# Gate and up projections in three plain passes, stage by stage, and a mixer input read row tile by row tile

## The chip, the cores and the metric

The kernel runs on one core of one Trainium2 chip. The metric is the device time of one execution in microseconds (us). Before the change it is 1038.3 us, the median of three runs (1037.62 to 1040.86 us). About 0.3% of that, some 3 us, is what a measurement can tell from no change.

## What is computed

A two-layer decoder trunk in float32 on 256 tokens of width 1024. Layer 0 is a half-step feed-forward, a Mamba-2 mixer, and a half-step feed-forward; layer 1 is a half-step feed-forward, a windowed attention over keys and values that were projected once, and a half-step feed-forward; a last norm follows. Cut to what matters:

```python
def swiglu(h, w_gate, w_up, w_down):
    return (jax.nn.silu(h @ w_gate) * (h @ w_up)) @ w_down
# D_MODEL = 1024, D_FF = 2816, SEQ = 256
x = x + 0.5 * swiglu(rmsnorm(x, norm_w[layer, 0]), gate0, up0, down0)
h = rmsnorm(x, norm_w[layer, 1])
x = x + mamba2_mixer(h, ...)            # layer 0: h @ w_in is 8 x 128 rows by 41 tiles of columns
x = x + swa_sink_attention(h, ...)      # layer 1
x = x + 0.5 * swiglu(rmsnorm(x, norm_w[layer, 2]), gate1, up1, down1)
```

The four feed-forward stages are called f0, f1, f2 and f3 in the program, in the order of time: f0 before the mixer, f1 and f2 between mixer and attention, f3 at the end.

## The kernel before

Every weight matrix is cut into units of 128 x 1024 (341 of them, in one fixed order, `ORDER`). `Weights` loads them two at a time over SyncE's queue; ScalarE rounds each to the type `fp32r` (`hi`, line 144), and VectorE makes the rest of it (`lo`, line 155). `tick()` (line 370), called after each unit's matmuls, runs what is due in a list of slots and then keeps the splitting four units ahead of TensorE. The activations are split in the same way: `xs[k]` is one tile of 128 x 512 whose left half is `xh[k]`, the high part of row tile k, and whose right half is `xl[k]`, the low part. A product keeps three of the four partial products: hi x xh, hi x xl, lo x xh.

There are two ways to work through a unit of the projections:

- `wide` (line 356): for each of eight row tiles k, one matmul of 512 columns (hi against xh and xl together) and one of 256 (lo against xh), so 16 matmuls. Its halves land side by side in one PSUM bank and have to be added: ScalarE copies the right half out, VectorE adds the left half (lines 513 to 515). With `by_part` (f > 0) the eight wide matmuls come first and the eight of 256 after them.
- `unit` (line 339): 24 matmuls of 256 columns into one half bank. Without `fresh` it runs hi x xh for all k, then hi x xl for all k, then lo x xh for all k. With `fresh` it goes row tile by row tile: for each k the three products together.

`ffn` (line 479) runs f = 0 to 21. Each f does the gate unit g, the up unit u, and from f = 4 on the down unit d of f - 4, in which `rows` (line 374) does 24 matmuls of 256 columns with the operands `hh` and `hl` that ScalarE and VectorE made of gate and up. The four down units that are left come at the end; the last two of them, in `tail` (line 542), are interleaved so that `next_stage` can take each finished row tile. In `product` (line 505) all units but the program's first go through `wide`. At the start of a stage the norm's sums go through TensorE after f = 0 (line 309) and its spread to all partitions after the gate of f = 1 (line 334). In f2, the two units of the shared keys (`kA`, `kB`) stand between u and d of f = 5.

`ssm` (line 550) reads its input with 41 units: `dt`, and then four B, four C, sixteen x and sixteen z. They go through `unit` into half banks named `sb`, with `fresh` for `dt` alone. Small matmuls and transposes of the mixer are slipped in between them. `att` (line 907) reads with `unit` too, with `fresh` for its first.

Of the kernel before, what the change touches and what calls it, by code (L numbers as in the profile page):

```python
# [17 lines left out]
T = 256  # L18
# [2 lines left out]
NF = 2816 // P  # L21
LAG = 4
SLACK = 2

NORM_AT = (1, 0, 0, 0)
SCALE_AT = (0, 0, 1, 0)
# [189 lines left out]
class Trunk:  # L216
# [262 lines left out]
    def ffn(self, l, i, key, nxt):  # L479
        nc, wk = self.nc, self.fw  # L480
        self.stage_norm(key)
        accs = self.accs(f"da_{key}")
        hs = {}

        def evac(f, g, u):
            hh = self.op.tile([P, T], F32R, tag="high", name=f"hh_{key}_{f}")
            hl = self.op.tile([P, T], F32R, tag="low", name=f"hl_{key}_{f}")
            hs[f] = (hh, hl)

            def e0():  # L490
                nc.vector.tensor_tensor(g, g, self.rs, ALU.mult)
                nc.scalar.activation(g, g, AF.Silu)
                nc.vector.tensor_tensor(u, u, self.rs, ALU.mult)

            def e1():
                nc.vector.tensor_tensor(u, u, g, ALU.mult)
                nc.scalar.activation(hh, u, AF.Copy)

            def e2():
                nc.vector.tensor_tensor(hl, u, hh.bitcast(F32), ALU.subtract)  # L500

            wait = max(0, 4 - f) if key == "f0" else 2 if f == 0 else 0
            self.slots.chain(wait, [e0, e1, e2])

        def product(name, f, t):

            b = self.bank(f"{name}_{key}_{f}")
            if self.W.pos == 0:
                self.slots.at(0, lambda: nc.scalar.copy(t, b[:, 0:T]))
                self.unit((name, l, i, f), b[:, 0:T])  # L510
                return

            def add():
                nc.scalar.copy(t, b[:, T:])  # L514
                nc.vector.tensor_tensor(t, b[:, 0:T], t, ALU.add)  # L515

            self.slots.at(0, add)
            self.wide((name, l, i, f), b, by_part=f > 0)

        for f in range(NF):  # L520
            g, u = (wk.tile([P, T], F32, tag=n, bufs=4, name=f"{n}s_{key}_{f}") for n in "gu")
            product("g", f, g)
            evac_now = lambda: evac(f, g, u)
            self.slots.late(0, evac_now)
            product("u", f, u)
            if l == 1 and i == 0 and f == 0:
                self.split_k()
            if l == 1 and i == 0 and f == 5:
                self.shared_k()
            if f >= LAG:  # L530
                self.down(l, i, f - LAG, hs, accs)
        for f in range(NF - LAG, NF - 2):
            self.down(l, i, f, hs, accs)
        self.tail([(("d", l, i, f), *hs.pop(f)) for f in (NF - 2, NF - 1)], accs, nxt)
# [15 lines left out]
    def ssm(self, nxt):  # L550
# [21 lines left out]
        def half():  # L572
            if st["n"] % 2 == 0:
                st["bank"] = self.bank(f"sb{st['n']}")
            o = st["bank"][:, (st["n"] % 2) * T : (st["n"] % 2) * T + T]
            st["n"] += 1
            return o

        def conv(c, out, o, d):
            u = ubufs[st["u"] % 4]  # L580
            st["u"] += 1

            def c0():
                V.tensor_tensor(u[:, 3:], o, self.rs, ALU.mult)

            def c1():
                A.activation(out, u[:, 3:], AF.Identity, scale=self.s("convw", 3 * 24 + c), bias=self.s("convb", c))

            def c2():
                pairs = st["taps"]  # L590
                pairs.append((out, u, c))
                if len(pairs) == 1:
                    sl.late(0, taps)

            def c3():
                A.activation(out, out, AF.Silu)

            sl.chain(d, [c0, c1, c2, c3])
# [69 lines left out]
        def cb(g):  # L668
            b = side(f"cb{g}")
            nc.tensor.matmul(b[:, 0:T], B[g][:, 0:P], C[g], start=True, stop=True)  # L670
            nc.tensor.matmul(b[:, T : T + P], B[g][:, P:T], C[g][:, P:T], start=True, stop=True)

            def e():
                m = wk.tile([P, 3, P], F32, tag="cbm", name=f"cbm{g}")
                V.tensor_tensor(m[:, 0], b[:, 0:P], causal, ALU.mult)
                V.tensor_tensor(m[:, 2], b[:, T : T + P], causal, ALU.mult)
                A.copy(m[:, 1], b[:, P:T])
                CB[g] = m

            sl.at(1, e)  # L680
# [22 lines left out]
        def prep(g):  # L703

            es = [wk.tile([P, 2, 3, P], F32, tag="E", bufs=6, name=f"E{4 * g + n}") for n in range(4)]

            def p0(n):
                tok = st["tok"]
                for i in range(2):
                    h = 8 * g + 2 * n + i  # L710
                    row = CSB[h // 4][:, h % 4]
                    A.activation(es[n][:, i, 0:2], row[:, 0:T], AF.Relu, bias=tok[:, 0, h : h + 1])
                    if i == 0:
                        V.tensor_scalar(es[n][:, i, 2], row[:, T:], tok[:, 1, h : h + 1], 0.0, ALU.add, ALU.max)
                    else:
                        A.activation(es[n][:, i, 2], row[:, T:], AF.Relu, bias=tok[:, 1, h : h + 1])

            def p1():
                for e in es:
                    A.activation(e, e, AF.Exp, scale=-1.0)  # L720

            def p2(n):
                f = es[n].rearrange("p n b l -> p n (b l)")
                c = CB[g].rearrange("p b l -> p (b l)").unsqueeze(1).broadcast_to([P, 2, 3 * P])
                V.tensor_tensor(f, f, c, ALU.mult)  # L725
                M[4 * g + n] = es[n]

            sl.chain(0, [lambda: p0(0), lambda: p0(1), lambda: p0(2), lambda: p0(3), p1])
            for n in range(4):
                sl.at(5 + n + DECAY_AT[g], lambda n=n: p2(n))  # L730
# [36 lines left out]
        def evac(what, o, d):  # L767
            kind = what[0]
            if kind == "dt":
                dt_chain(o, d)  # L770
            elif kind == "z":
                zs[what[1]] = z = wk.tile([P, T], F32, tag="zs", bufs=16, name=f"zs{what[1]}")
                sl.at(d, lambda: V.tensor_tensor(z, o, self.rs, ALU.mult))
                sl.at(d + 1, lambda: A.activation(z, z, AF.Silu))
            elif kind == "x":
                xs[what[1]] = x = wk.tile([P, T], F32, tag="xs", bufs=8, name=f"xs{what[1]}")
                conv(what[1], x, o, d)
            else:
                t = wk.tile([P, T], F32, tag=kind, name=f"{kind}{what[1]}")
                (B if kind == "B" else C)[what[1]] = t  # L780
                conv((16 if kind == "B" else 20) + what[1], t, o, d)
# [3 lines left out]
        at = {w: n for n, w in enumerate(seq)}  # L785
        ins = [w for w in seq if w[0] != "so"]

        E = {w: max(3, at[ins[min(i | 1, len(ins) - 1)]] + 1) for i, w in enumerate(ins)}
# [4 lines left out]
        for hg in range(8):  # L793
            g = hg // 2
            turned[hg] = max(E["x", 2 * hg], E["x", 2 * hg + 1]) + 3 + SLACK + TURN_AT[hg]
            if hg % 2 == 0:
                start[g] = max(free, turned[hg] - 5, E["C", g] + SLACK)
                free = start[g] + 7
            ymm_at[hg] = max(turned[hg] + 2, start[g] + 7 + 2 * (hg % 2)) + MIX_AT[hg]
        for g in range(GROUPS):  # L800
            plan(E["C", g] + 3 + SLACK, lambda g=g: cb(g))
            sl.at(base + start[g] - sl.now, lambda g=g: prep(g))
# [22 lines left out]
        for what in seq[:-2]:  # L825
            if what[0] == "so":
                tt = what[1]
                if not accs:
                    accs = self.accs("sa")
                self.rows([(self.W.next(what), yh[tt], yl[tt])], accs, tt == 0, False)  # L830
                self.tick()
            else:
                o = half()
                self.unit(what, o, before=lambda: evac(what, o, E[what] - at[what]), fresh=what == ("dt",))
        self.tail([(w, yh[w[1]], yl[w[1]]) for w in seq[-2:]], accs, nxt)


# [399 lines left out]
```

## Time and profile before

| What | us |
|---|---|
| median of three runs | 1038.3 |
| the profiled execution | 1038.29 |
| its span, first to last instruction | 1036.5 |
| TensorE busy | 1013.4 |
| VectorE busy | 774.7 |
| ScalarE busy | 627.4 |
| mean granted TensorE clock | 0.995 |

Of one execution the hardware profiler gives every instruction with its engine, its line and the names that it reads and writes. PE is TensorE's matmuls, PEld its weight loads, DVE VectorE, ACT ScalarE, POOL GpSimd, SP the queue that issues the DMAs. The program ran 1.8 us longer than its span. A matmul's start is recorded, its end is modelled; so the time of a group of matmuls is read here from one group's start to the next one's, and two groups overlap by a fraction of a microsecond in the listings. The chain of waits gives a group of equal matmuls on one line, with their count.

### The profile page before, as it was taken

The page shows a single profiled execution, that of the slowest core. Times are in us where ns is not written, and L with a number is a line of the kernel's source. Part 1 is how long each engine was busy: PE and PEld are TensorE (multiplying, and loading weights), DVE is VectorE, ACT ScalarE, POOL GpSimd, SP SyncE. Part 2 cuts the span into 40 slices and gives each one's busy share as a digit, 9 for nine tenths or more (in the row PEclk, how much of TensorE's full clock was granted, in tenths as well). Part 3 has the DMA queues.
Part 4 walks back from the last instruction along what each step waited for, and adds up shares of the span by engine and source line. Part 5 has one row for each costly group of instructions (what it writes and reads, how often), then busy time and mean ns, then how long its engine had stood idle before and what let it go on. Part 6 is the DMA issues. An engine that isn't in the chain of part 4 may idle for free.

```text
span 1036.5 us, 18344 instructions
## 1 busy us (share of the span) xinstructions
PE 1013.4 (98%) x7290; PEld 939.2 (91%) x7290; DVE 774.7 (75%) x1420; ACT 627.4 (61%) x1106; POOL 79.5 (8%) x122
## 2 busy tenths in 40 slices
PE   8999999999999999999999999999999999999996
PEld 7899999999989898999999899999998888999996
DVE  4866666888999968766667796666679877666665
ACT  6655555678886856555555664555565776555554
POOL 3000000210111112000000200000022020000000
PEclk9999999999999999999999999999999999999998
DMA  8555555547546354555455455555544335545531
GB/s 306 198 203 198 172 203 192 179 177 267 192 153 224 130 199 160 196 198 202 169 203 201 160 203 202 179 200 194 199 181 152 113 141 201 185 181 204 189 117 41
DMA packets 30132, 190.84 MB, mean 184 GB/s; under 512 B 3904, under 2 KB 5728, under 8 KB 8544
## 3 DMA queue, kind: packets, MB, share of 16 engines
q1 hardware_dynamic: 30048, 189.69, 51.5%
q8 instruction: 57, 0.93, 0.3%
q14 instruction: 27, 0.22, 0.1%
HBM read 187.27 MB, written 1.10 MB: 182 GB/s over the span
## 4 chain that ended last, share of the span: by engine, by line
PE 80%; DVE 12%; ACT 3%; DMA 2%; POOL 1%; issue 1%; SPq 0%; DVEq 0%; POOLq 0%
PE u_f L364 23%; PE g_f L364 22%; PE da_f L384 22%; PE sa L384 3%; PE sb L351 3%; DVE lo L155 2%; DVE xs L396 2%; PE aa L384 1%; DMA csb<-cs_scratch 1%; PE q L351 1%; DVE xs L603 1%; DVE X L404 1%; ACT hi L144 1%; DVE E L725 1%; ACT E L720 1%
## 5 line engine op out<-in xcount | busy, mean ns | idle before, releaser
L155 DVE TENSOR_TENSOR lo<-raw,hi 128x1024 fp32r<-128x1024 f32 (+1 forms) x343 | 414.9, 1213 | 15.2 <-ACT hi L144 15.2
L144 ACT ACTIVATE hi<-raw 128x1024 fp32r<-128x1024 f32 (+1 forms) x343 | 357.0, 1046 | 18.6 <-PE da_f L384 5.0
L384 PE MATMUL da_f<-hh_f,hi 128*128 128x256 f32 x704 | 194.3, 276 | 0.0
L384 PE MATMUL da_f<-hh_f,lo 128*128 128x256 f32 x704 | 194.3, 276 | 0.0
L384 PE MATMUL da_f<-hl_f,hi 128*128 128x256 f32 x704 | 194.3, 276 | 0.0
L364 PE MATMUL u_f<-xs,hi 128*128 128x512 f32 x704 | 181.2, 395 | 0.0
L364 PE MATMUL g_f<-xs,hi 128*128 128x512 f32 x696 | 176.6, 392 | 0.8 <-DVE xs L396 0.8
L364 PEld LDWEIGHTS u_f<-xs,hi 128*128 128x128 f32 x704 | 127.1, 188 | 22.4
L364 PEld LDWEIGHTS g_f<-xs,hi 128*128 128x128 f32 x696 | 124.5, 188 | 23.9 <-DVE xs L396 2.2
L384 PEld LDWEIGHTS da_f<-hl_f,hi 128*128 128x128 f32 x704 | 132.1, 188 | 0.0
L384 PEld LDWEIGHTS da_f<-hh_f,hi 128*128 128x128 f32 x704 | 132.1, 188 | 0.0
L384 PEld LDWEIGHTS da_f<-hh_f,lo 128*128 128x128 f32 x704 | 132.1, 188 | 0.0
L515 DVE TENSOR_TENSOR gs_f<-g_f,gs_f 128x256 f32<-128x256 f32 x87 | 37.0, 425 | 108.2 <-ACT gs_f L514 108.2
L364 PEld LDWEIGHTS u_f<-xs,lo 128*128 128x128 f32 x704 | 95.6, 189 | 7.3
L364 PEld LDWEIGHTS g_f<-xs,lo 128*128 128x128 f32 x696 | 95.4, 188 | 6.7
L515 DVE TENSOR_TENSOR us_f<-u_f,us_f 128x256 f32<-128x256 f32 x88 | 37.3, 424 | 85.0 <-ACT us_f L514 85.0
L364 PE MATMUL g_f<-xs,lo 128*128 128x256 f32 x696 | 99.6, 280 | 0.0
L364 PE MATMUL u_f<-xs,lo 128*128 128x256 f32 x704 | 99.6, 278 | 0.0
L514 ACT COPY us_f<-u_f 128x256 f32<-128x256 f32 x88 | 32.7, 372 | 107.5 <-PE u_f L364 107.5
L351 PE MATMUL sb<-xs,hi 128*128 128x256 f32 x656 | 87.0, 283 | 0.3 <-DVE xs L396 0.3
L514 ACT COPY gs_f<-g_f 128x256 f32<-128x256 f32 x87 | 32.2, 370 | 84.1 <-PE g_f L364 84.1
L351 PEld LDWEIGHTS sb<-xs,hi 128*128 128x128 f32 x656 | 80.9, 188 | 1.4 <-issue 0.5
(252 smaller groups left out, 1297.3 us busy)
## 6 DMA issues: line engine op xcount, KB each, us to landing
raw<-w SPq DMA_DIRECT2D x168, 1024.0 KB, 4.9
csb<-cs_scratch SPq DMA_DIRECT2D x8, 768.0 KB, 7.0
raw<-w SPq DMA_DIRECT2D x4, 512.0 KB, 7.7
X<-x SPq DMA_DIRECT2D x4, 256.0 KB, 5.8
Q<-r_q SPq DMA_DIRECT2D x32, 32.0 KB, 1.9
out<-o SPq DMA_DIRECT2D x3, 256.0 KB, 2.2
ca<-const_att SPq DMA_DIRECT2D x1, 704.0 KB, 6.2
raw<-w SPq DMA_DIRECT2D x2, 256.0 KB, 5.8
```

The costliest lines, as they stand in the source:

```text
L144: self.nc.scalar.activation(hi[:, s], self.chunks[c][:, i, s], AF.Copy)
L155: self.nc.vector.tensor_tensor(lo[:, s], self.chunks[c][:, i, s], hi[:, s].bitcast(F32), ALU.subtract)
L351: nc.tensor.matmul(out, w[:, k * P : (k + 1) * P], x[k], start=n == 0, stop=n == len(passes) - 1)
L364: self.nc.tensor.matmul(out[:, 0:c], w[:, k * P : (k + 1) * P], x[k], start=n == 0, stop=n == len(passes) - 1, skip_group_check=True,)
L384: nc.tensor.matmul(out, w[:, s], x, start=f and j < 4 and m == 0, stop=e and m == 2, skip_group_check=True)
L396: nc.vector.scalar_tensor_tensor(self.xl[j], self.X[j], wcol(j), self.xh[j].bitcast(F32), ALU.mult, ALU.subtract)
L404: nc.vector.scalar_tensor_tensor(self.X[j], out, scale, self.X[j], ALU.mult, ALU.add)
L514: nc.scalar.copy(t, b[:, T:])
L515: nc.vector.tensor_tensor(t, b[:, 0:T], t, ALU.add)
L603: V.scalar_tensor_tensor(out, u[:, tap : tap + T], self.s("convw", tap * 24 + c), out, ALU.mult, ALU.add)
L720: A.activation(e, e, AF.Exp, scale=-1.0)
L725: V.tensor_tensor(f, f, c, ALU.mult)
```

## The change

Two constants are added, one condition in `product`, and one argument in `ssm`:

```diff
+PLAIN = (("f0", "g"), ("f1", "u"), ("f2", "g"), ("f2", "u"), ("f3", "g"), ("f3", "u"))
+BY_ROW = ("f3",)
@@ def product(name, f, t)
             b = self.bank(f"{name}_{key}_{f}")
-            if self.W.pos == 0:
+            if self.W.pos == 0 or (f > 0 and (key, name) in PLAIN):
                 self.slots.at(0, lambda: nc.scalar.copy(t, b[:, 0:T]))
-                self.unit((name, l, i, f), b[:, 0:T])
+                self.unit((name, l, i, f), b[:, 0:T], fresh=key in BY_ROW and f > 0)
                 return
@@ def ssm(self, nxt)
                 o = half()
-                self.unit(what, o, before=lambda: evac(what, o, E[what] - at[what]), fresh=what == ("dt",))
+                self.unit(what, o, before=lambda: evac(what, o, E[what] - at[what]), fresh=True)
```

From f = 1 on, 21 gate units of f0, 21 up units of f1 and 42 units each of f2 and f3 go from `wide` to `unit`; in f3 these run row tile by row tile. ScalarE still copies the result out of PSUM, and VectorE's addition falls away. In the mixer the 40 units after `dt` take the order of `dt`.

## Rows read from the trace of the kernel before

**Rows 1.** The page: busy us of each engine, share of the span, instructions.
```profile
PE 1013.4 (98%) x7290; PEld 939.2 (91%) x7290; DVE 774.7 (75%) x1420; ACT 627.4 (61%) x1106; POOL 79.5 (8%) x122
```

**Rows 2.** Chain of waits, end of f0: start us, us, what, and count.
```profile
177.42 2.77 PE g_f L364 x16
180.19 2.74 PE u_f L364 x16
182.94 9.53 PE da_f L384 x84
...
196.69 0.33 DVE X L404
197.02 0.55 DVE xs L396
```

**Rows 3.** Timeline of TensorE, one f of f0: start us, us, line, what, count.
```profile
45.53 1.99 PE L364 MATMUL g_f<-xs,hi 128*128 128x512 f32 x8
47.35 1.11 PE L364 MATMUL g_f<-xs,lo 128*128 128x256 f32 x8
48.30 2.00 PE L364 MATMUL u_f<-xs,hi 128*128 128x512 f32 x8
50.13 1.07 PE L364 MATMUL u_f<-xs,lo 128*128 128x256 f32 x8
51.04 0.28 PE L384 MATMUL da_f<-hh_f,hi 128*128 128x256 f32 x1
```

**Rows 4.** Chain of waits in f2, around the units of the shared keys.
```profile
614.61 5.76 PE kab L351 x48
620.37 2.83 PE da_f L384 x24
623.20 2.79 PE g_f L364 x16
625.98 2.74 PE u_f L364 x16
```

**Rows 5.** Chain of waits in the mixer: the end of its output units.
```profile
373.88 15.56 PE sa L384 x132
```

**Rows 6.** Timeline of TensorE in the attention, after the norm's spread (line 334).
```profile
775.57 0.59 PE L334 MATMUL st_att<-dg_att,ones 128*128 128x256 f32 x2
775.82 2.24 PE L351 MATMUL q<-xs,hi 128*128 128x256 f32 x16
777.89 1.10 PE L351 MATMUL q<-xs,lo 128*128 128x256 f32 x8
778.83 0.40 PE L351 MATMUL q<-xs,hi 128*128 128x256 f32 x2
```

**Rows 7.** Timeline of TensorE at the mixer's first unit, row tile by row tile.
```profile
196.37 0.39 PE L351 MATMUL sb<-xs,hi 128*128 128x256 f32 x2
...
196.71 0.39 PE L351 MATMUL sb<-xs,hi 128*128 128x256 f32 x2
```

**Rows 8.** Timeline of TensorE in the attention's output units, after a score matmul.
```profile
821.93 0.28 PE L384 MATMUL aa<-ol,hi 128*128 128x256 f32 x1
...
822.27 0.28 PE L384 MATMUL aa<-ol,hi 128*128 128x256 f32 x1
```

**Rows 9.** The costliest groups, whole span: busy us, mean ns, idle before and releaser.
```profile
L515 DVE TENSOR_TENSOR us_f<-u_f,us_f 128x256 f32<-128x256 f32 x88 | 37.3, 424 | 85.0 <-ACT us_f L514 85.0
L364 PE MATMUL u_f<-xs,hi 128*128 128x512 f32 x704 | 181.2, 395 | 0.0
```

**Rows 10.** Timeline in the mixer: the shortest lead of a low part.
```profile
222.33 2.35 DVE L155 TENSOR_TENSOR lo<-raw,hi 128x1024 fp32r<-128x1024 f32 x2
228.70 2.13 PE L351 MATMUL sb<-xs,hi 128*128 128x256 f32 x16
```

**Rows 11.** Timeline of TensorE at the start of f0: the wait for the norm.
```profile
20.43 0.38 PE L309 MATMUL st_f<-ones,ss_in 128*128 128x1 f32 x2 [1.00 <-POOL ss_in L299]
```

**Rows 12.** One stretch at the start of f0: stretch, length, busy of engines, granted clock.
```profile
21.34:25.76 4.42, 4.42 (x18) 3.80 (x18) 3.97 (x6) 3.28 (x5) 1.24 (x1) 0.61 0.69 248
```

## The prediction

> **What bounds the kernel now.** I read the busy times first [rows 1], then the chain of waits, then TensorE's timeline. TensorE is busy 98% of the span, and in the feed-forward stages the chain is TensorE alone, one unit behind the other [rows 2]; its matmuls there sat idle for 0.0 us [rows 9]. So the feed-forward time is what TensorE takes for its units, and what VectorE or ScalarE save counts only where a stage begins or ends. The change leaves the columns alone: a wide unit streams 8 x 512 + 8 x 256 = 6144, a plain one 24 x 256 = 6144. What can differ is the pace, and for that the reader should compare matmuls of the same size. 256 columns come in two paces. Down units: 84 in 9.53 us, 113.5 ns each [rows 2]. The mixer's output units, the same loop over tiles of the same shape: 132 in 15.56 us, 117.9 ns [rows 5]. I call them fast and slow; 24 matmuls take 2.72 or 2.83 us.
>
> The pace is no property of the line; it is handed on. After the key units, which ran at 5.76 / 48 = 120 ns, a down unit of f2 takes 2.83 us [rows 4], where down units otherwise take 2.72. So a stream of 256-column matmuls keeps the pace that it finds, over the border between units too. The 512-column matmuls change it. The gate, which follows a fast down unit, has a slow narrow part: 48.30 - 47.35 = 0.95 us for eight. The up unit, which follows that slow part, ends fast: 51.04 - 50.13 = 0.91 us [rows 3]. So gate and up undo each other's step, and every down unit of the four stages runs fast, but for that one. One f now costs 2.77 + 2.74 + 2.72 = 8.23 us [rows 2].
>
> **What interrupts a stream, and what comes after.** Behind the attention's spread matmul (line 334) the stream of `unit` runs slow: eight in 778.83 - 777.89 = 0.94 us [rows 6]. That spread occurs six times in the trace with 256-column matmuls behind it (once for the mixer's norm, four times for its groups, once here), and all six streams behind it are slow. After the mixer's transposes and small products it is nearly always so too. The exception is [rows 8]: after one score product the output units run three in 0.34 us, fast.
>
> **The change part by part.**
>
> *f2, both plain.* The first plain gate follows f = 0, then comes the spread, then nothing but 256-column matmuls to the end of the stage, with no 512-column matmul that could turn the pace. By the six cases it starts slow and stays so; and even if it did not, the key units at f = 5 make it slow, which is the one thing that the trace shows in this very place [rows 4]. Gate: 21 x (2.83 - 2.77) = +1.3. Up: 21 x (2.83 - 2.74) = +1.9. Down: 21 x (2.83 - 2.72) = +2.3, since one is slow already. The last two down units are mostly covered: while they run, VectorE needs 0.33 + 0.55 = 0.88 us per finished row tile [rows 2] and TensorE 6 x 0.1135 = 0.68, slow 0.71, so the end of the stage is VectorE's; -0.2. Sum +5.3 us. If it were fast throughout: 21 x (-0.05 - 0.02) = -1.5.
>
> *f3, both plain, row tile by row tile.* The same spread, and no key units. The order by row tile is that of `rows`, which stays slow for 132 matmuls once it is slow [rows 5], so I give it no effect of its own. +1.3 + 1.9 + 22 x 0.11 = +5.6 us, with no cover at the end, where VectorE does less per row tile. If fast: -1.5.
>
> *f0, gate plain.* One wide unit per f is left, and it turns the pace once per f: fast, the up unit leaves slow; slow, it leaves fast. Gate and down in between hand the pace on. So the pace alternates from f to f. I count from the spread, which falls before the up unit of f = 2, and take the first turn as the present gate of f = 3 and up unit show it: 9 gates fast at -0.05, 11 slow at +0.06 (the gate of f = 1 ends in a wait of 1.00 us for the norm's sums [rows 11], which hides its 0.06); 9 up units that enter fast at +0.03; 13 down units slow at +0.11, less 0.2 of cover at the end. -0.5 + 0.7 + 0.3 + 1.2 = +1.7 us. Bounds: no turn and all fast, 21 x (2.72 + 2.77 + 2.72 - 8.23) = -0.4; all slow, 21 x 0.06 + 21 x 0.03 + 22 x 0.11 = +4.3. A turn can fail: after the slow down unit of f2 the gate took 2.79 us and the up unit was the one that ended fast [rows 4].
>
> *f1, up plain.* Likewise, the gate turning: 10 up units fast at -0.02, 11 slow at +0.09, 10 gates that enter slow at -0.03, 13 down units at +0.11, less 0.2: +1.7 us, with the same bounds.
>
> *The mixer's input, by row tile.* The 40 units after `dt` use the same 24 matmuls in another order. The low parts are wanted at the third matmul instead of the seventeenth, 14 x 0.118 = 1.65 us sooner; VectorE has them at least 228.70 - 224.68 = 4.0 us before the unit starts, counting from the end of the pair that holds the closest one [rows 10], so no wait comes of it. `dt` itself, in that order, ran at 0.34 us for three [rows 7], but it came behind fast down units and handed their pace on; the output units have that order and are slow. 0 us; fast it would be 40 x -0.11 = -4.4, and nothing in the trace makes it dearer than now.
>
> *VectorE and ScalarE.* 126 additions of 0.424 us [rows 9], 53 us of VectorE's 775, go. Worth 0: TensorE waits for none of them. In their place VectorE's next product by the norm (lines 491, 493) waits for ScalarE's copy itself. Behind it stand a product for `hl` and the splitting of weights, which runs four units (some 11 us) ahead. The DMA issues on SyncE follow the splitting and move by no more than the units do. Where an end of a stage is VectorE's, the last addition lies 13.6 us back.
>
> *The clock* falls once, to 0.61 in 4.42 us at the start [rows 12], after the wait for the norm [rows 11], which the change shortens by 0.06 us. A full clock there would give back 0.39 x 4.42 = 1.7 us; as much could be lost. I take 0.
>
> Sum: 1.7 + 1.7 + 5.3 + 5.6 = 14.3 us on the profiled 1038.29 (span 1036.5 and 1.8 around it; the median is 1038.3): **1052.6 us**. With the bounds of f0 and f1, 1048.5 to 1057.8.
>
> The rows show two paces at one column count, 113.5 and 117.9 ns [rows 2, 5]. The Trainium skill ("TensorE: Matmul & The Clock Gate", section "Back-to-back issue gap") has one: columns / 2.4 plus 2.5 ns. By that page a plain unit would take 24 x 109.2 = 2.62 us and a wide one 2.60, and the change would cost 126 x 0.02 = 2.5 us, 1040.8. The trace doesn't agree with it to the nanoseconds on which this case turns.
>
> **The rivals.**
> 1. *Slower, but the pace belongs to the kind of unit.* Plain units run at 2.83 as in the mixer, and down units stay at 2.72: 21 x (0.06 + 0.09 + 0.15 + 0.15) = +9.5, 1047.8 us. Against it: the slow down unit [rows 4].
> 2. *Row order is itself fast.* For it: `dt` [rows 7]. The mixer then gains 4.4, f3 1.5, the others as forecast: -4.4 - 1.5 + 1.7 + 1.7 + 5.3 = +2.8, 1041.1 us. Against it: the slow output units in row order [rows 5].
> 3. *Faster: streams without 512-column matmuls fall into the fast pace.* For it: the stream after the score product [rows 8]. It decides at one place, the first plain unit behind the spread in f2 and f3: if its matmuls come at 113 ns there and behind the key units too, f2 and f3 give -1.5 each, f0 and f1 -0.4 each, the mixer -4.4: -8.2, 1030.1 us. Against it: six streams out of six behind that spread.
> 4. *The additions matter, or the edit is idle.* `PLAIN` names keys that `ffn` really gets, so 126 units change. A gain by VectorE would have to show as TensorE waiting now, which it doesn't [rows 9].
>
> **How the numbers follow.** Forecast 0.62 (1048.5 to 1057.8), rival 1 0.10, rival 2 0.11, rival 3 0.14; rival 4 and the rest 0.03. A measurement tells 0.3%, 3.1 us, from no change. Slower: 0.62 + 0.10 + a little of the rest, 0.74; within, rival 2 and a little, 0.12; faster 0.14. From 1041.0 (just under rival 2) up to 1057.8 lie the forecast and rivals 1 and 2, 0.83.
>
> **What would show it.** In the profile after, matmuls of 256 columns in f2 and f3 near 118 ns, down units there 2.83 us; in f0 and f1 down units in turn 2.72 and 2.83; the mixer's input unchanged at 118. Plain units at 113 ns in f2 behind the key units would prove me wrong, and so would a mixer at 113.

## The result, and the profile after

The changed kernel takes 1051.65 us in the median (1050.33 to 1052.81), against 1039.3 (1037.62 to 1040.86; four runs, the three of 1038.3 and one more) for the kernel before on the same chip: 1.012 times as long, with a 95% interval of 1.0106 to 1.0134. The forecast was 1052.6, slower. The profiled execution after took 1052.69 (span 1050.9), 14.4 us over the profiled 1038.29 of before; the sum had been 14.3.

The page of after, busy times and one of the costliest groups (columns as in [rows 1] and [rows 9]). Lines have moved by 3 (`unit` is L354, `wide` L367, `rows` L387, the spread L337).

```profile
PE 1028.2 (98%) x8298; PEld 995.2 (95%) x8298; DVE 734.5 (70%) x1294; ACT 622.5 (59%) x1106; POOL 79.5 (8%) x122
...
L354 PE MATMUL u_f<-xs,hi 128*128 128x256 f32 x1008 | 146.1, 279 | 0.0
```

VectorE lost its 126 additions and 40 us, and ScalarE 5 us [rows 1]; TensorE, still 98% busy and still idle for 0.0 us ahead of its units, gained 1008 matmuls and 15 us. So the time went where the prediction looked for it: into the pace of TensorE's matmuls.

One f0 stretch of after in the chain of waits (start us, us, what, count), to be held against 2.77, 2.74 and 2.72 in [rows 2]:

```profile
45.59 2.72 PE g_f L354 x24
48.30 2.77 PE u_f L367 x16
51.08 2.83 PE da_f L387 x24
53.90 2.83 PE g_f L354 x24
56.73 2.74 PE u_f L367 x16
59.47 2.72 PE da_f L387 x24
...
183.93 9.91 PE da_f L387 x84
```

One f runs fast through the down unit and the plain gate, and its wide up unit leaves slow (2.77); the next runs slow (2.83 and 2.83), and its up unit leaves fast (2.74). The 84 matmuls of the last down units came out slow: 9.91 us for 9.53 [rows 2]. f1 does the same with the parts exchanged, from the spread on:

```profile
406.42 2.83 PE u_f L354 x24
409.24 2.74 PE g_f L367 x16
411.99 2.72 PE u_f L354 x24
414.70 2.77 PE g_f L367 x16
```

f2 of after, around the spread and around the key units; before, see [rows 4]:

```profile
588.10 2.83 PE g_f L354 x24
590.93 0.43 PE st_f L337 x2
591.36 2.83 PE u_f L354 x24
...
619.63 5.76 PE kab L354 x48
625.39 2.83 PE da_f L387 x24
628.22 2.83 PE g_f L354 x24
```

Every gate, up and down unit is at 2.83 us, before the key units as well as behind them; f3, row tile by row tile, is the same from its first plain gate to the 120 matmuls of its last five down units (14.13 us where before took 13.61). In both stages the gate ahead of the spread was slow already, so what the spread does is read from f1: the 256-column part of the gate ahead of it came at 113 ns from start to start, and the plain up unit behind it at 118. The mixer's input, now row tile by row tile, stands at 5.66 us for two units, 117.9 ns a matmul, the slow pace that [rows 6] showed behind the spread:

```profile
208.25 5.66 PE sb L354 x48
```

Where the 14.4 us lie, by stretches that run from a stage's first matmul to the next stage's: the mixer, f1 and f2 (stretch, length, busy us of PE, PEld, DVE, ACT and POOL with instructions, granted clock, DMA share, GB/s). After:

```profile
197.90:396.05 198.15, 191.21 (x1606) 184.65 (x1605) 173.12 (x332) 146.08 (x260) 29.94 (x52) 1.00 0.52 190
396.05:580.91 184.86, 184.63 (x1413) 176.66 (x1411) 123.82 (x197) 102.41 (x172) 7.21 (x12) 1.00 0.53 188
580.91:775.05 194.14, 193.89 (x1628) 192.85 (x1627) 126.38 (x192) 107.10 (x182) 9.76 (x14) 1.00 0.51 186
```

And before, the same stretches:

```profile
196.37:393.50 197.13, 190.78 (x1607) 184.63 (x1605) 173.50 (x332) 146.17 (x260) 30.07 (x53) 1.00 0.53 191
393.50:576.56 183.06, 182.81 (x1244) 167.92 (x1243) 130.53 (x218) 103.98 (x172) 7.10 (x11) 1.00 0.54 190
576.56:765.66 189.10, 188.84 (x1293) 173.80 (x1291) 138.64 (x234) 108.76 (x182) 9.75 (x14) 1.00 0.54 191
```

That is +1.02, +1.80 and +5.04. Read in the same way, f0 went from 188.54 to 190.64 (+2.10), f3 with the end from 194.77 to 199.76 (+4.99), the attention from 76.07 to 76.09, and the stretch ahead of f0 from 7.83 to 7.26. Together 14.4. In f1 and f2 TensorE is busy for all but 0.3 us of the stretch in both kernels, and the granted clock is 1.00 in both: the added time is neither a wait nor the clock.

### The profile page after: what moved, and what is told of

Same layout as the page of the kernel before. It is cut to its first block, busy times and chain, and to the rows that moved or that the text cites. A ratio compares the mean times of both kernels' runs of the same rounds, so it can differ in the third digit from the quotient of the medians.

```text
span 1050.9 us, 20219 instructions
## 1 busy us (share of the span) xinstructions
PE 1028.2 (98%) x8298; PEld 995.2 (95%) x8298; DVE 734.5 (70%) x1294; ACT 622.5 (59%) x1106; POOL 79.5 (8%) x122
## 4 chain that ended last, share of the span: by engine, by line
PE 80%; DVE 12%; ACT 3%; DMA 1%; POOL 1%; issue 1%; SPq 0%; DVEq 0%; POOLq 0%
PE da_f L387 22%; PE u_f L354 17%; PE g_f L354 16%; PE u_f L367 6%; PE g_f L367 6%; PE sa L387 3%; PE sb L354 3%; DVE lo L158 2%; DVE xs L399 2%; PE aa L387 1%; DVE xs L606 1%; PE q L354 1%; DVE X L407 1%; ACT hi L147 1%; DMA raw<-w 1%
## 5 line engine op out<-in xcount | busy, mean ns | idle before, releaser
L387 PE MATMUL da_f<-hh_f,hi 128*128 128x256 f32 x704 | 196.3, 279 | 0.0
L387 PE MATMUL da_f<-hh_f,lo 128*128 128x256 f32 x704 | 196.2, 279 | 0.0
L387 PE MATMUL da_f<-hl_f,hi 128*128 128x256 f32 x704 | 196.0, 278 | 0.0
L354 PE MATMUL g_f<-xs,hi 128*128 128x256 f32 x1024 | 150.4, 281 | 1.7 <-ACT hi L147 0.9
L354 PE MATMUL u_f<-xs,hi 128*128 128x256 f32 x1008 | 146.1, 279 | 0.0
L354 PEld LDWEIGHTS g_f<-xs,hi 128*128 128x128 f32 x1024 | 136.0, 189 | 3.3 <-ACT hi L147 1.4
L354 PEld LDWEIGHTS u_f<-xs,hi 128*128 128x128 f32 x1008 | 132.9, 188 | 0.2
L387 PEld LDWEIGHTS da_f<-hh_f,lo 128*128 128x128 f32 x704 | 132.3, 188 | 0.0
L387 PEld LDWEIGHTS da_f<-hh_f,hi 128*128 128x128 f32 x704 | 132.0, 188 | 0.0
L387 PEld LDWEIGHTS da_f<-hl_f,hi 128*128 128x128 f32 x704 | 132.0, 187 | 0.0
L354 PE MATMUL sb<-xs,hi 128*128 128x256 f32 x656 | 119.1, 283 | 0.1
L496 DVE TENSOR_TENSOR us_f<-us_f,rs_f 128x256 f32<-128x256 f32 x88 | 37.3, 423 | 110.4 <-ACT us_f L512 110.4
L354 PEld LDWEIGHTS sb<-xs,hi 128*128 128x128 f32 x656 | 100.4, 188 | 1.2 <-issue 0.5
L354 PE MATMUL g_f<-xs,lo 128*128 128x256 f32 x512 | 94.3, 280 | 0.0
L354 PE MATMUL u_f<-xs,lo 128*128 128x256 f32 x504 | 92.9, 279 | 0.0
L354 PE MATMUL sb<-xs,lo 128*128 128x256 f32 x328 | 91.6, 279 | 0.0
L512 ACT COPY us_f<-u_f 128x256 f32<-128x256 f32 x63 | 23.4, 372 | 87.7 <-PE u_f L354 87.7
L354 PEld LDWEIGHTS g_f<-xs,lo 128*128 128x128 f32 x512 | 75.1, 188 | 0.0
L354 PEld LDWEIGHTS u_f<-xs,lo 128*128 128x128 f32 x504 | 73.8, 188 | 0.0
```

What stands on the lines that cost most here:

```text
L354: nc.tensor.matmul(out, w[:, k * P : (k + 1) * P], x[k], start=n == 0, stop=n == len(passes) - 1)
L387: nc.tensor.matmul(out, w[:, s], x, start=f and j < 4 and m == 0, stop=e and m == 2, skip_group_check=True)
```

## Experiments

The theory: 256-column matmuls run at one of two paces, a stream hands its pace on across units, and only 512-column matmuls (or a break such as the spread or the key units) turn it. Two wide units in a row undo each other, one alternates, none leaves whatever was there. The rivals: the pace belongs to the kind of unit; the row order matters; more matmuls and weight loads cost time whatever their pace.

### The parts alone: e5_f23, e6_f01, e1_mixer

f2 and f3 plain, both in pass order, everything else as before:

```diff
-            if self.W.pos == 0:
+            if self.W.pos == 0 or (f > 0 and key in ("f2", "f3")):
```

> The kernel before with gate and up plain from f = 1 on in f2 and f3 alone, in f3 too in the order of passes and not row tile by row tile. Theory: these two stages carry 10.1 of the changed kernel's increase (5.0 in f2, 5.0 in f3, as its trace shows), every 256-column matmul in them at 117.8 ns whatever the order: +10 us, ratio 1.0097. Rival (the order by row tile matters in f3): f3 differs from the changed kernel's 5.0 us by over 1 us.

Measured: 1049.22 us (1048.29 to 1049.85), 1.0095 times before [1.008, 1.011]; +9.8 us. The units of f2 take 2.83 us here too. f3 had no row order in this kernel, and the loss is there all the same.

One plain product each in f0 and f1:

```diff
-            if self.W.pos == 0:
+            if self.W.pos == 0 or (f > 0 and (key, name) in (("f0", "g"), ("f1", "u"))):
```

> The kernel before with the gate of f0 and the up of f1 plain from f = 1 on, nothing else. Theory: down units alternate between 2.72 and 2.83 us; +1.7 in each stage against a before whose f0 runs gate slow, up fast, down fast (8.23 us per f). The run with the mixer alone showed f0 of before in the opposite step as well (gate fast, up slow, down slow, 8.34 us per f), which start it takes varying from one execution to the next; against that one f0 with a plain gate costs 22 x 0.11 - 1.7 = 0.7 us less. So between +1.0 and +3.4 us in the median, ratio 1.001 to 1.0033. Rival (the pace belongs to the kind of unit): +3.1 us with all down units at 2.72.

Measured: 1042.59 us (1041.85 to 1043.34), ratio 1.0034 [1.0021, 1.0047]; +3.2 us. The profile shows the alternation again, down units in turn 2.72 and 2.83. So the pace doesn't belong to the kind of unit. The two parts give 9.8 + 3.2 = 13.0 us, about the whole change's 12.4.

The mixer's input alone:

```diff
-                self.unit(what, o, before=lambda: evac(what, o, E[what] - at[what]), fresh=what == ("dt",))
+                self.unit(what, o, before=lambda: evac(what, o, E[what] - at[what]), fresh=True)
```

> The kernel before with one line of the change: the mixer's 40 input units after the first go row tile by row tile; the feed-forward stages are as before. My theory (the pace of 256-column matmuls is handed on, and their order does not matter): the mixer's input units stay at 117.8 ns per matmul and the time is that of before, 0 us within 1 us. In the changed kernel the mixer's stage came out 1.0 us longer (196.37 to 393.50 us before, 197.90 to 396.05 us after); if the row order is the cause of that, this run shows about +1 us in that stage, with waits of TensorE for VectorE's E and GpSimd's sums; if those waits came from elsewhere, it does not. Rival (row order is itself fast): 40 units at 113.3 ns, -4.3 us.

Measured: 1039.45 us in the median of ten runs (1037.52 to 1043.1), ratio 1.000 [0.9988, 1.0012]. The row order shows no effect on the time; the interval leaves room for 1.2 us either way. In the profiled execution, the slowest of the ten, the mixer's stretch took 199.06 us, 1.9 more than in the profile of before, where the expectation had put about +1 down to the row order if that is the cause; whether it is, is weighed below. What the run showed besides was not asked for. f0, which this kernel doesn't touch, ran in its profiled execution like this (chain of waits):

```profile
42.99 2.83 PE da_f L384 x24
45.81 2.74 PE g_f L364 x16
48.56 2.77 PE u_f L364 x16
```

In [rows 2] the gate leaves slow (2.77) and the up unit leaves fast (2.74). Here it is the other way round, and each down unit falls on the slow part. One f costs 2.74 + 2.77 + 2.83 = 8.34 us instead of 8.23, and f0 took 190.43 us instead of 188.54. The pace with which f0's stream begins is thus not fixed by the program.

### Even or odd: e2_even, e3_odd

If wide units turn the pace, a stage can be left fast for good by stopping them after the right one. Both products plain, but only from an f on at which the wide units before it have left the stream fast; in f2 both units of f = 6, behind the key units, stay wide to bring it back:

```diff
+PLAIN_FROM = {"f0": {"g": 4, "u": 4}, "f1": {"g": 2, "u": 2}, "f2": {"g": 2, "u": 2}, "f3": {"g": 3, "u": 3}}
+TURN = (("f2", "g", 6), ("f2", "u", 6))
...
-            if self.W.pos == 0:
+            if self.W.pos == 0 or (f >= PLAIN_FROM[key][name] and (key, name, f) not in TURN):
```

> The kernel before with gate and up both plain in all four stages, but only from the point at which the up unit of before leaves the stream fast: from f = 4 in f0, from 2 in f1 and f2, from 3 in f3; in f2 gate and up of f = 6, behind the key units, stay wide so that they turn the pace back. Theory (the pace is handed on and only 512-column matmuls turn it): every 256-column matmul from there to the end of its stage comes at 113.3 ns, each f saves 2.77 + 2.74 - 2 x 2.72 = 0.07 us, 18 + 20 + 19 + 19 of them: -5.3 us, so about 1034 where before is 1039.3, ratio 0.995. Rival (a plain unit is slow of itself, 2.83 us as in f2 and f3 of the changed kernel): 76 x (5.66 - 5.51) + down units = +11 to +20 us.

Measured: 1032.86 us in the median of twelve (1031.13 to 1040.22), ratio 0.9949 [0.993, 0.9967]: faster than both kernels of this case, with 152 plain units (f = 0 not counted) where the change has 126. Its chain of waits in f1, and behind the key units of f2:

```profile
407.43 2.76 PE u_f L366 x16
410.19 2.72 PE g_f L353 x24
```

```profile
616.43 5.76 PE kab L353 x48
622.19 2.83 PE da_f L386 x24
625.02 2.79 PE g_f L366 x16
627.80 2.74 PE u_f L366 x16
630.54 2.72 PE da_f L386 x24
```

Plain units at 2.72, down units at 2.72, 8.16 us for one f. Behind the keys it takes two wide units: the first stays slow, the second leaves fast. Three of the twelve runs lie at 1038 to 1040. The profiled execution was one of them (1038.41), and shows where it lost: f0, and f0 alone, was left slow by its last wide unit, since it had begun in the other step, and it stayed slow for the rest of the stage (chain, f0):

```profile
31.42 2.74 PE g_f L366 x16
34.16 2.77 PE u_f L366 x16
36.94 2.83 PE g_f L353 x24
```

f0 took 193.14 us there. Where the other two of the three lost was not looked at. Now one wide unit less in each stage, and one less behind the key units:

```diff
+PLAIN_FROM = {"f0": {"g": 4, "u": 3}, "f1": {"g": 2, "u": 1}, "f2": {"g": 2, "u": 1}, "f3": {"g": 3, "u": 2}}
+TURN = (("f2", "g", 6),)
```

> The same as the run with even turns, but one more up unit per stage is plain (f = 3 in f0, 1 in f1 and f2, 2 in f3, and f = 6 in f2), so that the last wide unit ahead of the plain stream is a gate, which leaves it slow. Five units of 341 differ between the two. Theory (the pace is handed on): every 256-column matmul of those streams at 117.8 ns, 2.83 us for gate, up and down: 5.0 us in f0 and 5.3 us in each of f1, f2 and f3, +21 us against before, 26 us against the run with even turns. Rival (the pace belongs to the kind of unit): the two runs differ by less than 1 us.

Measured: 1058.54 us (1058.08 to 1058.67), ratio 1.0181 [1.0168, 1.0194]; +19.2 against the 21 expected. All four stages run at 2.83 throughout. Five units more out of 176 made plain, and the time is 25.7 us above that of the kernel before it: neither the number of matmuls or weight loads, nor the additions, nor the order within a unit explains that. The pace that the last wide unit hands on does.

### The count of 512-column matmuls: e4_six

Wide units with six matmuls of 512 columns instead of eight, the columns kept (the other two row tiles by four of 256):

```diff
+SIX = 6
...
-            passes = passes[0::2] + passes[1::2]
+            passes = [(k, hi, self.xs, 2 * T) for k in range(SIX)]
+            passes += [(k, hi, x, T) for k in range(SIX, KT) for x in (self.xh, self.xl)]
+            passes += [(k, lo, self.xh, T) for k in range(KT)]
```

> The kernel before, all gate and up units from f = 1 on with 512-column matmuls for six of their eight row tiles and 256-column ones for the other two: 6 of 512, then 4 of 256 for the high parts, then 8 of 256 for the low part. The starts of before's 512-column matmuls come in a cycle of three (226, 229, 232 ns), and a stream leaves fast where the last step was the 232 one. Theory (the count modulo three decides): six are two whole cycles, so a unit leaves the stream as it found it, gate and up have the same pace throughout a stage, either fast (8.19 us per f, -0.04 against before) or slow (8.40 us, +0.17) according to how the spread left it; no down unit alternates. Between -3.4 us (all four fast) and +14 us (all slow). Rival (any run of 512-column matmuls turns the pace): narrow parts of gates slow, of ups fast, as before, 8.25 us per f and within 2 us of before.

Measured: 1048.84 us (1048.13 to 1049.67), ratio 1.0089 [1.0075, 1.0102]. Chain of waits in f2, on both sides of the key units:

```profile
618.63 2.80 PE u_f L367 x18
621.43 5.76 PE kab L352 x48
627.18 2.83 PE da_f L387 x24
630.01 2.75 PE g_f L367 x18
632.76 2.73 PE u_f L367 x18
635.49 2.72 PE da_f L387 x24
```

There is no alternation left: f0, f1, f3 and the first part of f2 are slow from the spread on and stay so (2.79 or 2.80 for gate and up, 2.83 for down). Behind the key units the first unit of six turns the stream fast, where a unit of eight did not (2.79 in `e2_even`), and it stays fast to the stage's end. So eight turn the pace and six keep it, and slow is not one state: the slow stream behind the keys reacts to both counts otherwise than the usual one. The same two lines ran slow ahead of the keys and fast behind them: the stream carries the pace, no line owns it.

### Forcing f0's start: e7_sync

The kernel `e2_even` with two more matmuls of 256 columns, whose result is not used, behind a plain gate of f0 and a six-wide up unit after them, meant to turn f0 fast where it began in the other step; the gate of f = 6 in f2 has six too:

```diff
+SIX = (("f0", "u", 4), ("f2", "g", 6))
+SHIFT = ("f0", "g", 4)
...
+        for _ in range(2 if spare is not None else 0):
+            nc.tensor.matmul(spare, lo[:, 0:P], xh[0], start=True, stop=True, skip_group_check=True)
```

> The run with even turns, made independent of how f0 starts. Of that run's 12 executions three took 1038 to 1040 us and the others 1031 to 1035, and its profile, one of the three, has f0 slow throughout. Here the gate of f = 4 in f0 is plain with two more 256-column matmuls behind it (into an unused half bank, their result is not used), and the up unit of f = 4 has six 512-column matmuls; in f2 the gate of f = 6 has six and its up is plain. Theory (a fast stream is left fast by 256-column matmuls and by six of 512; a slow one is moved by two matmuls to the step from which six of 512 leave it fast, as behind the key units in the run with six): f0 is fast from the up unit of f = 4 in every execution, none at 1038 or over, median 1031 to 1034, ratio about 0.994. Rival (the two matmuls and the count of six have no such effect): a quarter of the executions again at 1038 to 1040, or f0 slow in the profile.

Measured: 1033.73 us in the median of eight (1033.09 to 1039.87), ratio 0.9955 [0.9939, 0.997]. Seven runs lie within 1033.1 and 1034.5, and one at 1039.87, which the expectation had excluded. That one is the profiled execution. f0 was fast in it, but it had come in fast, so the added matmuls had nothing to turn; f1 was the slow one (chain, f1):

```profile
398.95 2.77 PE g_f L371 x16
401.73 0.43 PE st_f L337 x2
402.16 2.78 PE u_f L371 x16
404.94 2.83 PE g_f L354 x24
```

In `e2_even` the up unit behind this spread took 2.76 us and left the stream fast; here it took 2.78 and left it slow. The 256-column part of the gate ahead of the spread shows the difference already: 118 ns from start to start here, 113 in `e2_even` and in the kernel before. So f1's start varies as well. The miss is one of scope: f0 is not the only place that isn't fixed. Whether the added matmuls turn an f0 that comes in slow is not shown by this run: one slow execution in eight here and three in twelve in `e2_even` do not tell the two kernels apart.

### Two matmuls that turn a slow stream: e8_two_more, e9_none_more

The odd kernel, slow in every stage, with the two unused matmuls and a six-wide up unit at five places (one in each stage, and a second in f2 behind the keys), and the same without the two:

```diff
+SIX = (("f0", "u", 4), ("f1", "u", 2), ("f2", "u", 2), ("f2", "u", 7), ("f3", "u", 3))
+SHIFT = (("f0", "g", 4), ("f1", "g", 2), ("f2", "g", 2), ("f2", "g", 7), ("f3", "g", 3))
+MORE = 2
```

> The run with odd turns, whose streams were slow to the end of every stage, with five places changed: behind a plain gate (f = 4 in f0, 2 in f1, 2 and 7 in f2, 3 in f3) stand two more 256-column matmuls into an unused half bank (their result is not used), and the up unit after it has six 512-column matmuls instead of none. Theory: a slow stream goes through three steps, each 256-column matmul moves it by one, and two more bring it to the step from which six 512-column matmuls end on the 232 one; the stream is fast from there to the end of the stage, 2.72 us per unit. With the few slow units ahead of each place and 5 x 0.23 us for the added matmuls: -3 us against before, ratio 0.997, some 22 us below the run with odd turns. Rival (six of 512 leave a slow stream slow whatever stands before): ratio 1.018 as the run with odd turns. A stage where it fails costs 5.3 us, and its profile shows which.

> The same with the six 512-column matmuls in those five up units, but without the two more 256-column matmuls ahead of them. Theory: the slow stream comes to the up unit at the step at which six of 512 leave it slow, as in the run with six in f1 and f3: all streams slow, ratio 1.018, like the run with odd turns (the five units themselves take 2.79 instead of 2.83 us). Rival (it is the six matmuls alone, or their position, that turns it): ratio 0.997 like the run with two more.

Measured: with the two, 1040.94 us (ten runs, 1034.47 to 1043.85), ratio 1.0011 [0.9991, 1.0032], where 0.997 was expected; without them 1056.47 (1050.74 to 1056.72), 1.0152 [1.012, 1.0185]. f0 with the two (chain of waits; L358 is the pair):

```profile
37.86 2.83 PE g_f L356 x24
40.69 0.23 PE g_f L358 x2
40.92 2.75 PE u_f L373 x18
43.67 2.72 PE da_f L393 x24
```

And without:

```profile
36.85 2.83 PE g_f L356 x24
39.68 2.79 PE u_f L373 x18
```

Ten matmuls that compute nothing of use, some 1.2 us of TensorE's time, make the kernel 15.5 us faster. Without them none of the five places turned in the profiled execution (one of the four runs took 1050.74, 5.7 less than the others, about the 5.3 that one stage is worth; it was not profiled). With them four of five did; the first one in f2 did not, though the place in f1, behind the same units, did. First f1, then f2:

```profile
402.17 2.76 PE g_f L373 x16
...
411.25 2.75 PE u_f L373 x18
```

```profile
584.37 2.79 PE g_f L373 x16
...
593.24 0.24 PE g_f L358 x2
593.48 2.79 PE u_f L373 x18
```

f2 stayed slow up to the key units. The two stages differ in how they began: the wide gate ahead of the spread (the first line of each) left f1 fast and f2 slow. In `e9_none_more` it was f1 that began slow and f2 that began fast. The time between the starts of the first two 512-column matmuls of the six-wide unit goes with that. In a stage that began fast it was 230 ns without the two added matmuls (f2) and 235 with them (f1); 235 also stands behind the key units in `e4_six`, where six turn the stream fast. In a stage that began slow it was 233 without them (f1) and 229 with them (f2), and from either six left the stream slow. So the two matmuls moved the stream in both stages, but only from one of the two starts to the step that suits; the miss came from the stage's start, which the program does not fix. That rests on one execution of each kernel. The direction of the whole is as the theory wants it, the size is not: the runs spread over 9 us. Other starts in other executions would explain the spread, but only one execution was looked at, so that is argued and not shown.

## Why the prediction was right, and where it was off

**The pace is handed on, and wide units turn it.** Right, and the runs bear it: +25.7 us between the odd and the even kernel, and 15.5 us from ten idle matmuls. Rival 1 (the pace belongs to the kind of unit) falls with the down units that alternate in f0 and f1. Rival 2 (the row order is fast) falls with the mixer's input at 117.9 ns, and with f3. Rival 3 (plain streams fall into the fast pace) falls in f2 and f3, which stay slow to the end behind the spread. What hands the pace on inside the chip no run shows.

**f2 and f3: +5.3 and +5.6 forecast, +5.04 and +4.99 measured.** The mechanism is the forecast one; the terms were slightly large, since they are differences of rows rounded to hundredths, taken some 20 times each. The 120 matmuls of the last five down units of f3 give the difference with less rounding: (14.13 - 13.61) / 5 = 0.104 us for 24 matmuls, where 0.11 was used. From the start of f3's gate of f = 1 to the end of its down units it is 176.13 before and 181.35 after, +5.2; the rest of the shortfall is 0.2 at the stage's beginning, which I had not looked for.

**f0: +1.7 forecast, +2.10 measured.** From the gate of f = 3 to the mixer 164.60 became 166.38, +1.78, which is the term; the stretch ahead of it, with the norm's waits, became 0.3 longer. The cover at the end was there: the stage's last row tiles belong to VectorE in both kernels.

**f1: +1.7 forecast, +1.80 measured.** The count of fast and slow units by alternation held, here and in f0: 9 fast gates in f0, 10 fast up units in f1, and 13 slow down units in each.

**The mixer: 0 forecast, +1.02 in the profiled execution, 0 in the runs.** The input units kept their pace. The stretch varies by itself: in pass order it took 196.3 to 199.2 us over nine profiles, and in row order 198.15 and 199.06, longer than eight of the nine. In the waits of the profile after, the one that grew most is for the transfer of `csb`, a tile that the mixer reads back from memory: VectorE's `E` waited 3.9 us for it where before 2.6. Since the change of the mixer alone came out at 1.000 [0.9988, 1.0012], the 1.02 isn't put down to the row order; a part of it may be.

**The additions: 0 forecast, and 0 found.** The additions' own rows lost the 53 us that were counted (74.3 to 20.8), VectorE's busy time as a whole 40, and TensorE had waited for none of it [rows 9].

**The clock: 0 forecast.** The granted clock dips once at the start in both; where it was 0.61 in the stretch of 21.34 to 25.76 us [rows 12], it is 1.00 after, and the dip has moved to 12 to 17 us (0.69). The start of f0 up to the gate of f = 3 took 23.94 and 24.26 us, so nothing came of it.

**What the prediction took as fixed and is not.** "Every down unit of the four stages runs fast, but for that one" holds for the execution that was profiled. In another one f0 ran with all down units slow, 1.9 us longer, with the same instructions. The starts of f1, f2 and f3 vary too (last section), but there the gate and up units that follow bring both starts to the same alternation as long as all of them are wide: in the profile of before f1 began fast and f3 slow, and both had all their down units fast.

**How good the sum is.** That it fits from profile to profile (14.3 and 14.4) is in part luck: f0, f1, the mixer and the attention came out 1.5 us above their terms together, f2 and f3 0.9 below theirs, and the stretch ahead of f0, for which there was no term, 0.6 shorter. In the medians the change is 12.4 us, 2 less than the sum. The profiled execution of before lies 1.0 us under the median of its kernel's four runs, that of after 1.0 over its own; the prediction set a profiled time beside a median as if they were the same thing. How much of these 2 us is the start of f0 was not measured.

**Slips in the working.** The terms of f0 and f1 at their lower bounds give 1048.4, not 1048.5, and with f1's own terms the upper bound of f1 is 21 x 0.09 - 21 x 0.03 + 22 x 0.11 = +3.7, not f0's +4.3. The fast stream of [rows 8] is not the only exception: the output units behind the product at 830.74 us in the attention came at 113 ns too. None of this changes the forecast.

The estimate by the formula of the Trainium skill ("TensorE: Matmul & The Clock Gate", section "Back-to-back issue gap") had been 1040.8 us. The measured 1051.65 and the two paces in the rows don't agree with it at this precision: streams of the same form ran at 2.72 and 2.83 us for 24 matmuls, where it has one value. The section itself gives the formula for an isolated matmul, and says that in a stream of weight loads and matmuls both set the spacing; every matmul here has its weight load, so the estimate used the formula outside of what it is given for.

## What to carry to other kernels

When TensorE is busy nearly all the time, compare the time of matmuls of one size between stages, and between units of one stage, before trusting that equal columns mean equal time: 4% lay here between two streams of the same instructions. If the pace is handed on, the question about an edit is not how many columns it moves but what pace it leaves behind for the next hundred units, and one more or one fewer unit of the other shape can decide it. Look at more than one execution of such a kernel: what sets the pace at a stage's start may vary where the program doesn't.

## What the runs showed of the hardware that was not expected

A stream of 256-column matmuls has more than two states. Start to start they took 113.3 ns or 117.8 ns, and 120 in the key units. 512-column matmuls start 226, 229 and 232 ns apart in a repeating cycle of three. From a fast stream, eight of 512 leave it slow and six leave it fast. From the usual slow stream eight leave it fast, and six leave it slow. From the other slow one, behind the key units, eight leave it slow, and six leave it fast. The first two starts of 512-column matmuls tell the two slow streams apart: 229 or 230 ns behind the usual one, 235 behind the other. A third slow stream shows 233 or 234, in f1 of `e9_none_more` and in f0 and the first part of f2 of `e4_six`, and six leave it slow. Two more matmuls of 256 columns ahead of six turned the slow stream fast at four places out of five, with 235 at the four, and 229 at the one that stayed slow. A cycle of three steps of which one suits the 256-column matmuls would be in keeping with all that; what in the chip makes the steps was not tested and stays open.

A stage that begins with the same instructions begins in one step in some executions and in another in others. f0 did so in two of the eight profiles whose units around its spread are those of before (`e1_mixer`, `e2_even`). In the other stages, whose spread stands one f earlier than f0's, the gate ahead of the spread had its 256-column part at 113 ns in some profiles and at 118 in others; where this gate is the wide one of eight, it was 118 three times in ten in f1, three in eight in f2 and five in eight in f3. `e2_even` took 1031.1 to 1035.0 us nine times and 1038.4 to 1040.2 three times. What decides the start is open too. The place of the clock's dip alone doesn't, for f0: it lay at 12 to 17 us both in the execution of the mixer's kernel that began f0 in the other step and in that of the changed kernel that began as forecast.
